# Causal attention: the value step by groups of four query tiles instead of pairs

## The chip, the cores and the metric

The kernel runs on one core of one Trainium2 chip. The metric is the device time of one execution in microseconds; the kernel before stands at 2201.59 us, the median of 3 runs.

## The reference

One layer of a decoder: a half-step feed-forward block, one input projection, three branches (spatial gating, causal multi-head attention, attention into a memory), a gated merge, and a second half-step feed-forward block. Batch 1, 1024 positions, model width 1024, all in float32. The change touches only the causal attention, which has 8 heads with queries and keys of 96 and values of 64 columns:

```python
def causal_block_attention(q, k, v):
    ...
    scale = Dqk ** -0.5
    ...
        s = jnp.einsum('bqhd,bkhd->bhqk', qi, k).astype(jnp.float32) * scale
        qpos = i * Q_BLOCK + jnp.arange(Q_BLOCK)
        mask = kpos[None, :] <= qpos[:, None]
        s = jnp.where(mask[None, None], s, NEG)
        p = jax.nn.softmax(s, axis=-1)
        return jnp.einsum('bhqk,bkhd->bqhd', p.astype(v.dtype), v)
```

## The kernel before, in words

**Precision.** A float32 operand of a matmul is split into a high part `hi` (a cast on ScalarE, ACT, line 127) and a low part `lo` (a subtraction on VectorE, DVE, line 128) by `split`. A product of two split operands is three matmuls on TensorE, PE (`mm3`, lines 144 to 146). The value step is an exception: the 128 stationary columns of `vv` hold the high and the low part of a head's 64 value columns side by side, so that two matmuls do, one with the high and one with the low part of the probabilities, and two halves of the result are added afterwards.

**Tiles.** The 1024 positions are 8 tiles of 128. A head is worked in four steps j = 0 to 3 of two query tiles each, i = 2j and 2j + 1, and all eight heads follow one another; the stage lies at about 1286 to 1431 us of the profiled span.

- `scores(h, j)`, line 838: for each of the two query tiles, `mm3` against the keys that the mask allows, into a tile `mm` of two PSUM banks; on DVE a reduction that adds the mask, takes the maximum and writes the scores to SBUF as `pr0` to `pr7` (line 857: a custom instruction of 128 x 128(i + 1) and a short one that reads the accumulator into `a_mx`); on ACT the exponential in place (line 863), which also leaves the row sums in `a_rs`. There is one buffer for each `pr`.
- `turn(h, j)`, line 867: the probabilities are transposed on PE (line 879), up to four tiles of 128 x 128 into one PSUM bank, and split (line 885) into buffers `whi` and `wlo`. Step j has j + 1 such blocks, each with two key tiles times two query tiles. In the last block one of the four tiles lies beyond the mask: it isn't transposed, and POOL writes zeros there (line 884).
- `value(h, j)`, line 889: 2j + 2 key tiles, for each a matmul with the high and one with the low part, 256 moving columns each (lines 894 and 895), accumulated in a bank. ACT copies one half of the result to `ysum` (line 902), DVE adds the other half (line 903). After every second step of an odd head four query tiles of two heads are complete: DVE takes the reciprocal of the row sums (`a_inv`, line 908), POOL spreads it, PE transposes it (line 914), ACT copies it (916), POOL multiplies (917), and the result is split (919).
- `prepare(h + 1)`, line 823: the next head's queries and keys are transposed (line 415, tiles `aq` and `ak`), four transposes to a block, and split with a gain (lines 136 and 137).

**Buffers.** PSUM has 8 banks: `bank` is a pool of four (turned blocks, prepare, value sums, transposed reciprocals), and `mm` has two tiles of two banks. `whi` and `wlo` have five buffers each, with room for two blocks in each.

**Order.** Each engine works through its instructions in order, and the program's order is the order in which this code calls the functions, refined by a scheduler that places the instructions of nearby calls by estimated times. Step n of the loop (line 925) calls `scores` of step n, up to two blocks of `prepare`, `turn` of step n - 1 and `value` of step n - 2.

Of the kernel before, what the change touches and what calls it, by code (L numbers as in the profile page):

```python
# [8 lines left out]
F32 = mybir.dt.float32  # L9
# [7 lines left out]
P = 128  # L17
# [3 lines left out]
NT = S // P  # L21
# [4 lines left out]
H = 8  # L26
# [16 lines left out]
class Kernel:  # L43
# [756 lines left out]
    def attention(self):  # L800

        nc, tc = self.nc, self.tc
# [12 lines left out]
        yt, st, qkt, pair, ysum, inv = [], {}, {}, {}, {}, {}  # L815
        with tc.tile_pool(name="att", bufs=1) as p:
# [50 lines left out]
            def turn(h, j):  # L867
                prs, out = st[h, j], []
                for c in range(j + 1):
                    if c % 2 == 0:  # L870
                        hi, lo = (self.wide(n).rearrange("p (c q) -> p c q", c=2) for n in ("whi", "wlo"))
                    b = self.bank()

                    order = (2 * c + 1, 2 * c)
                    for s, kk in enumerate(order):
                        for t in range(2):
                            if kk <= 2 * j + t:
                                at = (2 * s + t) * P
                                nc.tensor.transpose(b[:, at:at + P], prs[t][:, kk * P:(kk + 1) * P], self.ident)  # L879
                    dst = hi[:, c % 2], lo[:, c % 2]  # L880
                    z = P if c == j else 0
                    if z:
                        for x in dst:
                            nc.gpsimd.memset(x[:, :z].bitcast(F32), 0.0)
                    self.split(dst[0][:, z:], dst[1][:, z:], b[:, z:])
                    out += [(kk, tuple(x[:, s * 2 * P:(s + 1) * 2 * P] for x in dst)) for s, kk in enumerate(order)]
                st[h, j] = out

            def value(h, j):
                o = self.bank()[:, :2 * P]  # L890
                pts = st.pop((h, j))
                for n, (kk, pt) in enumerate(pts):
                    w = vv[kk][:, h].rearrange("p s d -> p (s d)")
                    nc.tensor.matmul(o, w, pt[0], start=n == 0, stop=False)  # L894
                    nc.tensor.matmul(o, w, pt[1], start=False, stop=n == len(pts) - 1)  # L895
                own = h % 2 * VD
                rows, other = slice(own, own + VD), slice(VD - own, 2 * VD - own)
                if h % 2 == 0 and j % 2 == 0:
                    ysum[h // 2, j // 2] = p.tile([P, 4 * P], F32, name="ysum", bufs=3)
                ys = ysum[h // 2, j // 2]  # L900
                y = ys[rows, j % 2 * 2 * P:(j % 2 + 1) * 2 * P]
                nc.scalar.copy(y, o[other])
                nc.vector.tensor_tensor(y, y, o[rows], op=ALU.add)
                if h % 2 and j % 2:
                    b = self.bank()
                    w = self.row()
                    rs = self.small.tile([P, 2, 4], F32, name="a_inv", tag="a_inv")
                    nc.vector.reciprocal(rs, inv[h // 2][:, :, 2 * (j - 1):2 * (j + 1)])
# [9 lines left out]
                    cols = slice((j - 1) * 2 * P, (j + 1) * 2 * P)  # L918
                    self.split(yt[h // 2][0][:, cols], yt[h // 2][1][:, cols], ys)

            steps = [(h, j) for h in range(H) for j in range(NT // 2)]
# [3 lines left out]
            for n in range(len(steps) + 2):  # L925
                if n < len(steps):
                    h, j = steps[n]
                    scores(h, j)
                    if j == 0 and h + 1 < H:
                        ahead = prepare(h + 1)  # L930
                    for _ in range((0, 2, 1, 2)[j]):
                        next(ahead, None)
                if 0 <= n - 1 < len(steps):
                    turn(*steps[n - 1])
                if n >= 2:
                    value(*steps[n - 2])
# [999 lines left out]
```

## Time and profile before

| | |
|---|---|
| runs | 2201.34, 2201.59, 2202.05 us |
| median | 2201.59 us |
| span of the profiled execution | 2198.6 us |
| the profiled execution's own time | not given beside its span; the median of the runs lies 3.0 us above the span |
| PE, busy share of the span | 99% |
| DVE | 70% |
| ACT | 41% |
| POOL | 11% |

"Busy" counts an engine's instructions and not its waits. PE's instructions overlap, so that their durations add up to more than the time they take; what one of them costs is read from the distance between starts. An operand is written as out<-in by the program's names, with partitions x elements behind it. A row of a group of instructions ends with the idle time ahead of them and with the instruction that ended most of it. A row of the timeline has the time from the span's start, the duration, the engine, the line, and how many equal instructions stand together. In the table of stretches each engine has its busy time and, in brackets, its instructions; the last three numbers are PE's granted clock, the share of DMA and GB/s.

### The profile page before, as it was taken

To read this page: it belongs to the slowest core of one execution; us is meant where nothing else is said; L and a number is where in the kernel's file an instruction comes from. 1 tells how busy PE (TensorE), PEld (TensorE's weight loads), DVE (VectorE), ACT (ScalarE), POOL (GpSimd) and SP (SyncE) were. 2 spreads that over 40 slices of the span, in tenths; PEclk is the share of its full clock that TensorE was granted. 3 is DMA by queue.
4 is the path that set the end of the run, shared out by engine and by line. 5 is a ranking of instruction groups with operands and counts; after the bars stand their busy time and mean duration, and the time that the engine had idled before them with its cause. 6 is when DMAs were issued, how large, how long until landed. Compare 5 with 4: busy or idle time off the path is not lost.

```text
span 2198.6 us, 27597 instructions
## 1 busy us (share of the span) xinstructions
PE 2181.6 (99%) x10304; PEld 1819.9 (83%) x10304; DVE 1549.2 (70%) x2415; ACT 896.7 (41%) x1501; POOL 243.8 (11%) x246
## 2 busy tenths in 40 slices
PE   9999999999999999999999999999999999999999
PEld 5788888888887888898888889988888888888887
DVE  7966666679889555467466769885886666657884
ACT  5422222243455333444244559843432222234332
POOL 0012112100000000022000221140011111210000
PEclk9999999999999999999999999999999999999999
DMA  4242333385432333225151541094033333338543
GB/s 145 82 146 99 96 101 115 133 306 172 133 114 96 125 106 125 94 92 172 55 190 58 218 175 43 17 332 166 29 124 100 99 109 101 115 116 299 170 130 106
DMA packets 113062, 285.92 MB, mean 130 GB/s; under 512 B 13344, under 2 KB 21664, under 8 KB 112800
## 3 DMA queue, kind: packets, MB, share of 16 engines
q1 hardware_dynamic: 112928, 284.16, 38.0%
q8 instruction: 81, 1.33, 0.2%
q14 instruction: 53, 0.43, 0.1%
HBM read 201.80 MB, written 82.31 MB: 129 GB/s over the span
## 4 chain that ended last, share of the span: by engine, by line
PE 93%; DVE 5%; ACT 1%; issue 1%; DMA 0%; SPq 0%; ACTq 0%; DVEq 0%
PE bank L144 13%; PE bank L145 13%; PE bank L146 13%; PE one L144 13%; PE one L145 13%; PE one L146 13%; PE mm L146 3%; PE mm L144 3%; PE mm L145 3%; PE bank L879 1%; PE bank L415 1%; PE bank L894 1%; PE bank L895 1%; DVE wlo L133 1%; PE one L1579 1%
## 5 line engine op out<-in xcount | busy, mean ns | idle before, releaser
L132 ACT CAST whi<-x 128x1024 fp32r<-128x1024 f32 (+1 forms) x189 | 179.5, 952 | 469.8 <-PE one L145 206.8
L1283 DVE TENSOR_TENSOR t<-t,one 128x512 f32<-128x512 f32 x178 | 122.2, 686 | 229.5 <-PE one L146 228.7
L144 PE MATMUL bank<-h,whi 128*128 128x512 f32 x644 | 250.9, 390 | 0.0
L145 PE MATMUL bank<-h,whi 128*128 128x512 f32 x644 | 250.7, 389 | 0.0
L146 PE MATMUL bank<-h,wlo 128*128 128x512 f32 x644 | 250.5, 389 | 0.0
L133 DVE TENSOR_TENSOR wlo<-x,whi 128x1024 fp32r<-128x1024 f32 (+1 forms) x189 | 226.2, 1198 | 28.6 <-ACT whi L132 28.5
L144 PE MATMUL one<-h,whi 128*128 128x512 f32 x476 | 186.2, 391 | 0.7 <-ACT t L1392 0.7
L146 PE MATMUL one<-h,wlo 128*128 128x512 f32 x476 | 185.2, 389 | 0.0
L145 PE MATMUL one<-h,whi 128*128 128x512 f32 x476 | 185.2, 389 | 0.0
L127 ACT CAST whi<-w 128x1024 fp32r<-128x1024 f32 (+1 forms) x108 | 95.1, 899 | 143.4 <-PE one L145 62.7
L128 DVE TENSOR_TENSOR wlo<-w,whi 128x1024 fp32r<-128x1024 f32 (+1 forms) x108 | 110.1, 1033 | 60.5 <-ACT whi L127 60.4
L144 PE MATMUL one<-w,whi 128*128 128x512 f32 x392 | 152.5, 389 | 0.0
L145 PE MATMUL one<-w,whi 128*128 128x512 f32 x392 | 152.5, 389 | 0.0
L146 PE MATMUL one<-w,wlo 128*128 128x512 f32 x392 | 152.5, 389 | 0.0
L1680 POOL TENSOR_TENSOR raw<-raw 128x512 f32<-128x512 f32 x38 | 62.6, 1647 | 804.3 <-DVE raw L1526 804.3
L146 PEld LDWEIGHTS bank<-h,wlo 128*128 128x128 f32 x644 | 120.9, 188 | 25.1
L144 PEld LDWEIGHTS bank<-h,whi 128*128 128x128 f32 x644 | 120.9, 188 | 24.9
L145 PEld LDWEIGHTS bank<-h,whi 128*128 128x128 f32 x644 | 120.9, 188 | 24.8
L144 PE MATMUL bank<-whi 128*128 128x512 f32 x352 | 136.9, 389 | 0.0
L145 PE MATMUL bank<-wlo,whi 128*128 128x512 f32 x352 | 136.9, 389 | 0.0
L146 PE MATMUL bank<-whi,wlo 128*128 128x512 f32 x352 | 136.9, 389 | 0.0
L128 DVE TENSOR_TENSOR wlo<-h,whi 128x512 fp32r<-128x512 f32 x130 | 88.2, 714 | 25.7 <-ACT whi L127 25.7
(381 smaller groups left out, 5040.1 us busy)
## 6 DMA issues: line engine op xcount, KB each, us to landing
x<-in_ffn_w_gu_dram SPq DMA_DIRECT2D x78, 512.0 KB, 5.1
w<-tdt SPq DMA_DIRECT2D x40, 512.0 KB, 4.8
tdb<-raw SPq DMA_DIRECT2D x64, 256.0 KB, 2.1
h<-in_ffn_w_down_dram SPq DMA_DIRECT2D x64, 256.0 KB, 6.0
w<-tdb SPq DMA_DIRECT2D x30, 512.0 KB, 4.5
tdt<-w SPq DMA_DIRECT2D x48, 256.0 KB, 2.1
gate<-raw SPq DMA_DIRECT2D x23, 512.0 KB, 2.6
tdt<-raw SPq DMA_DIRECT2D x40, 256.0 KB, 2.9
```

The source lines that it names most:

```text
L127: self.nc.scalar.copy(hi, src)
L128: return (eng or self.nc.vector).tensor_tensor(lo, src, hi.bitcast(F32), op=ALU.subtract)
L132: self.nc.scalar.copy(hi, src)
L133: return lambda: self.nc.vector.tensor_tensor(lo, src, hi.bitcast(F32), op=ALU.subtract)
L144: mmul(out, s[0], m[0], start=first, stop=False, **kw)
L145: mmul(out, s[0], m[1], start=False, stop=False, **kw)
L146: self.last = mmul(out, s[1], m[0], start=False, stop=last, **kw)
L415: nc.tensor.transpose(b[:m, k * P:(k + 1) * P], s, self.ident)
L879: nc.tensor.transpose(b[:, at:at + P], prs[t][:, kk * P:(kk + 1) * P], self.ident)
L894: nc.tensor.matmul(o, w, pt[0], start=n == 0, stop=False)
L1283: return self.nc.vector.tensor_tensor(out, x, y, op=ALU.add)
L1680: sub = lambda d, x, y: (eng or nc.gpsimd).tensor_tensor(d, x, y, op=ALU.subtract)
```

## The change

`turn` and `value` now work on groups g of four query tiles (4g to 4g + 3) in place of pairs. `blocks(g)` lists what is turned together into one bank: for each of the key tiles 0 to 4g, all four query tiles (512 columns); then key tile 4g + 1 for the query tiles 1 to 3 together with key tile 4g + 3 for query tile 3 (384 + 128 columns); then key tile 4g + 2 for the query tiles 2 and 3 (256 columns). Group 1 has seven blocks, named b0 to b6 below, group 0 has three, b0' to b2'. Nothing beyond the mask is stored, so the zeros go. The value matmuls take 512 columns, or 384, 256 or 128 where the mask cuts. The sum of a group stays in one bank, which may be kept from one call of `value` to the next. `ysum` is copied and added in 512 columns.

A step j of head h now calls, behind `scores` and `prepare`: for j = 0 the blocks b0 to b2 of the head before; for j = 1 its b3 to b6 and the value matmuls of its first four key tiles; for j = 2 the rest of these, and the three blocks of head h's group 0; for j = 3 the value matmuls of group 0. Per head 36 transposes and ten splits of turned probabilities stay; the value matmuls of all eight heads fall from 320 to 192.

```diff
@@ -812,7 +812,7 @@
                     src = raw[:, t].rearrange("p (x o d) -> p x o d", o=2, d=VD)[:, :, o]
                     d = v.rearrange("p (x o) s d -> p x o s d", o=2)[:, :, o]
                     self.split(d[:, :, o], d[:, :, 1 - o], src)
-        yt, st, qkt, pair, ysum, inv = [], {}, {}, {}, {}, {}
+        yt, st, qkt, pair, ysum, inv, ptt, acc, room = [], {}, {}, {}, {}, {}, {}, {}, []
         with tc.tile_pool(name="att", bufs=1) as p:
             self.causal_mask(p)
 
@@ -864,48 +864,52 @@
                         pr[:, :n], pr[:, :n], ACT.Exp, bias=mx[:, t:t + 1], scale=-1.0, accum_out=rs[:, t:t + 1])
                 st[h, j] = prs
 
-            def turn(h, j):
-                prs, out = st[h, j], []
-                for c in range(j + 1):
-                    if c % 2 == 0:
-                        hi, lo = (self.wide(n).rearrange("p (c q) -> p c q", c=2) for n in ("whi", "wlo"))
-                    b = self.bank()
-
-                    order = (2 * c + 1, 2 * c)
-                    for s, kk in enumerate(order):
-                        for t in range(2):
-                            if kk <= 2 * j + t:
-                                at = (2 * s + t) * P
-                                nc.tensor.transpose(b[:, at:at + P], prs[t][:, kk * P:(kk + 1) * P], self.ident)
-                    dst = hi[:, c % 2], lo[:, c % 2]
-                    z = P if c == j else 0
-                    if z:
-                        for x in dst:
-                            nc.gpsimd.memset(x[:, :z].bitcast(F32), 0.0)
-                    self.split(dst[0][:, z:], dst[1][:, z:], b[:, z:])
-                    out += [(kk, tuple(x[:, s * 2 * P:(s + 1) * 2 * P] for x in dst)) for s, kk in enumerate(order)]
-                st[h, j] = out
-
-            def value(h, j):
-                o = self.bank()[:, :2 * P]
-                pts = st.pop((h, j))
-                for n, (kk, pt) in enumerate(pts):
+            def blocks(g):
+
+                return [[(kk, 0, 0)] for kk in range(4 * g + 1)] + [
+                    [(4 * g + 1, 1, 0), (4 * g + 3, 3, 3 * P)], [(4 * g + 2, 2, 0)]]
+
+            def turn(h, g, some):
+                prs, out = st[h, 2 * g] + st[h, 2 * g + 1], ptt.setdefault((h, g), [])
+                for n in some:
+                    if n % 2 == 0:
+                        room[:] = [self.wide(x).rearrange("p (c q) -> p c q", c=2) for x in ("whi", "wlo")]
+                    b, at = self.bank(), 0
+                    for kk, t0, at in blocks(g)[n]:
+                        for t in range(t0, 4):
+                            nc.tensor.transpose(b[:, at:at + P], prs[t][:, kk * P:(kk + 1) * P], self.ident)
+                            at += P
+                    dst = [x[:, n % 2] for x in room]
+                    self.split(dst[0][:, :at], dst[1][:, :at], b[:, :at])
+                    out += [(kk, t0, [x[:, c:c + (4 - t0) * P] for x in dst]) for kk, t0, c in blocks(g)[n]]
+
+            def value(h, g, n=None):
+                pts, total = ptt[h, g], 4 * g + 4
+                if (h, g) not in acc:
+                    acc[h, g] = self.bank(), []
+                o, done = acc[h, g]
+                for kk, t0, pt in pts[:n]:
                     w = vv[kk][:, h].rearrange("p s d -> p (s d)")
-                    nc.tensor.matmul(o, w, pt[0], start=n == 0, stop=False)
-                    nc.tensor.matmul(o, w, pt[1], start=False, stop=n == len(pts) - 1)
+                    for x in pt:
+                        done.append(nc.tensor.matmul(
+                            o[:, t0 * P:], w, x, start=not done, stop=len(done) == 2 * total - 1))
+                del pts[:n]
+                if len(done) < 2 * total:
+                    return
+                del acc[h, g]
                 own = h % 2 * VD
                 rows, other = slice(own, own + VD), slice(VD - own, 2 * VD - own)
-                if h % 2 == 0 and j % 2 == 0:
-                    ysum[h // 2, j // 2] = p.tile([P, 4 * P], F32, name="ysum", bufs=3)
-                ys = ysum[h // 2, j // 2]
-                y = ys[rows, j % 2 * 2 * P:(j % 2 + 1) * 2 * P]
+                if h % 2 == 0:
+                    ysum[h // 2, g] = p.tile([P, 4 * P], F32, name="ysum", bufs=3)
+                ys = ysum[h // 2, g]
+                y = ys[rows]
                 nc.scalar.copy(y, o[other])
                 nc.vector.tensor_tensor(y, y, o[rows], op=ALU.add)
-                if h % 2 and j % 2:
+                if h % 2:
                     b = self.bank()
                     w = self.row()
                     rs = self.small.tile([P, 2, 4], F32, name="a_inv", tag="a_inv")
-                    nc.vector.reciprocal(rs, inv[h // 2][:, :, 2 * (j - 1):2 * (j + 1)])
+                    nc.vector.reciprocal(rs, inv[h // 2][:, :, 4 * g:4 * g + 4])
                     for o in range(2):
                         d = rs[:, o].unsqueeze(2)
                         nc.gpsimd.tensor_copy(
@@ -915,25 +919,32 @@
                     w = self.row()
                     nc.scalar.copy(w, b)
                     nc.gpsimd.tensor_tensor(ys, ys, w, op=ALU.mult)
-                    cols = slice((j - 1) * 2 * P, (j + 1) * 2 * P)
+                    cols = slice(g * 4 * P, (g + 1) * 4 * P)
                     self.split(yt[h // 2][0][:, cols], yt[h // 2][1][:, cols], ys)
 
-            steps = [(h, j) for h in range(H) for j in range(NT // 2)]
             ahead = prepare(0)
             for _ in ahead:
                 pass
-            for n in range(len(steps) + 2):
-                if n < len(steps):
-                    h, j = steps[n]
-                    scores(h, j)
-                    if j == 0 and h + 1 < H:
-                        ahead = prepare(h + 1)
-                    for _ in range((0, 2, 1, 2)[j]):
-                        next(ahead, None)
-                if 0 <= n - 1 < len(steps):
-                    turn(*steps[n - 1])
-                if n >= 2:
-                    value(*steps[n - 2])
+            for h in range(H + 1):
+                for j in range(NT // 2):
+                    if h < H:
+                        scores(h, j)
+                        if j == 0 and h + 1 < H:
+                            ahead = prepare(h + 1)
+                        for _ in range((0, 2, 1, 2)[j]):
+                            next(ahead, None)
+                    if h and j == 0:
+                        turn(h - 1, 1, range(3))
+                    elif h and j == 1:
+                        turn(h - 1, 1, range(3, 7))
+                        value(h - 1, 1, 4)
+                    elif j == 2:
+                        if h:
+                            value(h - 1, 1)
+                        if h < H:
+                            turn(h, 0, range(3))
+                    elif j == 3 and h < H:
+                        value(h, 0)
         return yt
 
     def mixer(self, norm):

```

The scheduler's order moves with it. Three places follow, each as one engine's rows in the order of the program; "x2" stands for two equal instructions in a row.

On DVE, between the first and the last reduction of the query tiles 4 to 7 of one head, after the change (`pr_10998` to `pr_11083` are the tiles pr4 to pr7; the splits `wlo` are those of the turned blocks of the head before, `x_10477` the attention's result, `h_10943` a prepared key or query):

```order
L907 TENSOR_TENSOR ysum<-ysum,bank 64x512
L128 TENSOR_TENSOR wlo<-bank,whi 128x512 x3
L857 ISA pr_10998,a_mx<-mm,mask 128x640
L857 ISA a_mx 128x1
L128 TENSOR_TENSOR x_10477<-ysum,x_10476 128x512
L857 ISA pr_11007,a_mx<-mm,mask 128x768
L857 ISA a_mx 128x1
L137 SCALAR_TENSOR_TENSOR h_10943<-bank,g_ev_k,h_10942 96x512
L128 TENSOR_TENSOR wlo<-bank,whi 128x512 x3
L857 ISA pr_11074,a_mx<-mm,mask 128x896
L857 ISA a_mx 128x1
L857 ISA pr_11083,a_mx<-mm,mask 128x1024
```

The same engine and place before the change (`pr_11093` to `pr_11155` are pr4 to pr7, the splits are those of the same head's tiles 2 to 5):

```order
L903 TENSOR_TENSOR ysum<-ysum,bank 64x256
L857 ISA pr_11093,a_mx<-mm,mask 128x640
L857 ISA a_mx 128x1
L857 ISA pr_11102,a_mx<-mm,mask 128x768
L857 ISA a_mx 128x1
L128 TENSOR_TENSOR wlo<-bank,whi 128x512 x2
L857 ISA pr_11146,a_mx<-mm,mask 128x896
L857 ISA a_mx 128x1
L128 TENSOR_TENSOR wlo<-bank,whi 128x512
L128 TENSOR_TENSOR wlo<-bank,whi 128x384
L857 ISA pr_11155,a_mx<-mm,mask 128x1024
L857 ISA a_mx 128x1
```

Before, pr4 and pr5 are reduced one behind the other; after, splits of group 1 of the head before stand ahead of pr4, between pr4 and pr5 and between pr5 and pr6. Since the turned blocks of that group read its old pr4 to pr7, the new pr4 can be written only when the transposes of b0 to b4, which read the old one, are done.

On PE, at the end of a head's group 1 after the change (`h_10418` to `h_10421` are the value columns of the key tiles 4 to 7, `pr_10655` to `pr_10701` the tiles pr0 to pr3 of the next head, `aq` its successor's queries):

```order
L894 MATMUL bank<-whi,h_10418 128x512
L415 MATMUL bank<-ident,aq 96x128 x4
L894 MATMUL bank<-wlo,h_10418 128x512
L894 MATMUL bank<-whi,h_10419 128x384
L894 MATMUL bank<-wlo,h_10419 128x384
L894 MATMUL bank<-whi,h_10421 128x128
L894 MATMUL bank<-wlo,h_10421 128x128
L894 MATMUL bank<-whi,h_10420 128x256
L880 MATMUL bank<-ident,pr_10655 128x128
L880 MATMUL bank<-ident,pr_10661 128x128
L880 MATMUL bank<-ident,pr_10695 128x128
L880 MATMUL bank<-ident,pr_10701 128x128
```

The end of a value step of query tiles 4 and 5 on PE before (the same names; `h_10541` to `h_10544` are the next keys and queries):

```order
L894 MATMUL bank<-whi,h_10419 128x256
L895 MATMUL bank<-wlo,h_10419 128x256
L894 MATMUL bank<-whi,h_10418 128x256
L895 MATMUL bank<-wlo,h_10418 128x256
L415 MATMUL bank<-ident,ak 96x128 x4
L144 MATMUL mm<-h_10543,h_10541 128x512
L145 MATMUL mm<-h_10544,h_10541 128x512
L146 MATMUL mm<-h_10543,h_10542 128x512
```

After the change the value matmuls of one head stand in long runs, with the widths 512, 384, 128 and 256 at the end, and the transposes of b0' (key tile 0 for pr0 to pr3) follow them; before, runs of value matmuls of 256 columns alternate with scores.

On DVE at the end of the last head after the change (`pr_12196` and `pr_12205` are pr6 and pr7):

```order
L857 ISA pr_12196,a_mx<-mm,mask 128x896
L857 ISA a_mx 128x1
L128 TENSOR_TENSOR wlo<-bank,whi 128x256
L857 ISA pr_12205,a_mx<-mm,mask 128x1024
L857 ISA a_mx 128x1
L912 RECIPROCAL a_inv<-a_rs 128x8
L128 TENSOR_TENSOR wlo<-bank,whi 128x512 x2
L907 TENSOR_TENSOR ysum<-ysum,bank 64x512
L128 TENSOR_TENSOR wlo<-bank,whi 128x256
```

The same place before (`pr_12417` and `pr_12426` are pr6 and pr7):

```order
L857 ISA pr_12417,a_mx<-mm,mask 128x896
L857 ISA a_mx 128x1
L903 TENSOR_TENSOR ysum<-ysum,bank 64x256
L857 ISA pr_12426,a_mx<-mm,mask 128x1024
L857 ISA a_mx 128x1
L128 TENSOR_TENSOR wlo<-bank,whi 128x384
L908 RECIPROCAL a_inv<-a_rs 128x8
L903 TENSOR_TENSOR ysum<-ysum,bank 64x256
L128 TENSOR_TENSOR wlo<-bank,whi 128x512
L128 TENSOR_TENSOR wlo<-bank,whi 128x384
```

The reciprocal stood behind one split of the last head and now stands directly behind the last reduction, ahead of all the splits of group 1 and of the add of `ysum`.

## The prediction, made before the changed kernel ran

> **What bounds the kernel now.** I read the page first, for the engine that carries the end.
> ```profile
> span 2198.6 us, 27597 instructions
> PE 2181.6 (99%) x10304; PEld 1819.9 (83%) x10304; DVE 1549.2 (70%) x2415; ACT 896.7 (41%) x1501; POOL 243.8 (11%) x246
> PE 93%; DVE 5%; ACT 1%; issue 1%; DMA 0%; SPq 0%; ACTq 0%; DVEq 0%
> ```
> PE carries 93% of the chain that ended last, so a microsecond saved on PE is a microsecond of time, provided PE stays fed. Averages over the whole kernel say little about the attention, so I next read the table of stretches for two windows inside it (columns: length, then busy time and instructions of PE, PEld, DVE, ACT, POOL, then granted clock and DMA).
> ```profile
> 1340.00:1360.00 20.00, 20.00 (x151) 18.89 (x151) 18.37 (x43) 16.84 (x38) 3.56 (x11) 1.00 0.03 13
> 1400.00:1420.00 20.00, 19.98 (x151) 18.62 (x151) 18.31 (x42) 17.26 (x41) 3.74 (x15) 1.00 0.01 2
> ```
> Here PE has no gap, but DVE is busy 92% and ACT 84 to 86%. This is the point on which the whole prediction turns: the stage is bound by PE with almost no slack on the two engines that feed it. The clock is 1.00 and no DMA matters.
>
> **What one instruction costs.** PE's matmuls overlap, so their price is the distance from start to start in the timeline, not the duration.
> ```profile
> 1394.75 1.80 PE L879 MATMUL bank<-ident,pr 128*128 128x128 f32 x15
> 1396.31 0.48 PE L144 MATMUL mm<-h,h 96*128 96x512 f32 x1
> 1396.62 0.40 PE L145 MATMUL mm<-h,h 96*128 96x512 f32 x1
> 1396.86 0.39 PE L146 MATMUL mm<-h,h 96*128 96x512 f32 x1
> 1397.08 0.34 PE L144 MATMUL mm<-h,h 96*128 96x384 f32 x1
> 1397.26 0.34 PE L145 MATMUL mm<-h,h 96*128 96x384 f32 x1
> ...
> 1399.00 0.28 PE L894 MATMUL bank<-whi,h 128*128 128x256 f32 x1
> 1399.12 0.28 PE L895 MATMUL bank<-wlo,h 128*128 128x256 f32 x1
> ```
> A matmul of 512 columns takes 0.23 us (1396.62 to 1396.86, to 1397.08), one of 384 takes 0.175 (1397.08 to 1397.26, rounded), one of 256 takes 0.12. The 15 transposes take 1.56 us, and the matmul behind them holds the next one 0.08 longer than usual (0.31): (1.56 + 0.08) / 15 = 0.11 each.
>
> **The change on PE: fewer, wider value matmuls.** Before, a head's value step has 2 + 4 + 6 + 8 = 20 key tiles, each with a hi and a lo matmul of 256 columns: 320 in all, 320 x 0.12 = 38.4 us. After, a head has 12 key tiles: six of 512 columns and two each of 384, 256 and 128. That is 96 x 0.23 = 22.1, 32 x 0.175 = 5.6, 32 x 0.12 = 3.8, and 32 of 128 columns, which the trace before doesn't have.
> ```profile
> L895 PEld LDWEIGHTS bank<-wlo,h 128*128 128x128 f32 x136 | 25.9, 190 | 0.1
> ```
> No row fits, so I bound it: at least 0.06 (half of the 256-column matmul), at most 0.19 (the whole weight load, if nothing hid it). I take 0.11, the transposes' spacing, the nearest row with 128 columns and a weight load of its own: 3.5 us. The sum is 35.0, a gain of **3.4 us** on PE (5.0 and 0.8 at the ends). The Trainium skill (TensorE: Matmul & The Clock Gate, Back-to-back issue gap) gives about 81 ns for a weight load and matmul pair of 128 columns, which would make the gain 4.3. The same place gives 131 ns for 512 columns, where this trace has 230, so I don't lean on it.
>
> The transposes stay 36 per head, and the scores are untouched. So per head PE has before: 56 transposes (36, 16 of prepare, 4 of the sums) x 0.11 = 6.2, scores 18 x 0.23 + 6 x 0.175 + 12 x 0.12 = 6.6, value 4.8, together 17.6; after, 17.2.
>
> **The change on DVE, ACT and POOL.**
> ```profile
> L128 DVE TENSOR_TENSOR wlo<-bank,whi 128x512 fp32r<-128x512 f32 x41 | 26.9, 677 | 2.1 <-POOL wlo L884 2.1
> L127 ACT CAST whi<-bank 128x512 fp32r<-128x512 f32 x41 | 22.6, 578 | 0.1
> L128 DVE TENSOR_TENSOR wlo<-bank,whi 128x384 fp32r<-128x384 f32 x27 | 14.7, 545 | 0.0
> L903 DVE TENSOR_TENSOR ysum<-ysum,bank 64x256 f32<-64x256 f32 x26 | 10.8, 415 | 1.6 <-ACT ysum L902 0.8
> L902 ACT COPY ysum<-bank 64x256 f32<-64x256 f32 x26 | 9.5, 366 | 4.3 <-PE bank L895 3.2
> ```
> A head has ten splits of turned probabilities before and after, and 4608 columns in both (6 x 512 + 4 x 384; now 8 x 512 + 2 x 256): no change. The memsets on POOL go; the first row says that DVE waited 2.1 us for them in 120, beside a PE without gaps, so I cost them at nothing. The 32 copies and adds of ysum become 16 of twice the width. By the pair 384 to 512 the step of 128 columns is 0.13 us on DVE, so an add of 512 takes about 0.415 + 0.26 = 0.68, and DVE saves 2 x 0.415 - 0.68 = 0.15 each, 2.4 us in all; ACT about as much. That is 0.3 us per head on engines with about 1.5 to spare: useful, but PE doesn't wait for their sum, it waits for their order.
>
> **The order, which is the real question.** Before, a step turns two query tiles; turning, value and scores alternate finely. After, seven blocks of group 1 (b0 to b6) are turned in one go beside steps 0 to 2 of the next head, three blocks (b0' to b2') of group 0 in step 2. I walked PE, ACT and DVE by hand through the order of the changed program with these rows; t = 0 is the first score of query tile 4 of an odd head.
> ```profile
> 1341.26 0.81 DVE L857 CUSTOM_DVE_ANT_0 pr<-mm,mask 128x640 f32<-128x640 f32 x1
> 1342.00 0.08 DVE L857 DVE_READ_ACCUMULATOR2_ANT a_mx<- 128x1 f32 x1
> ...
> 1342.67 0.94 DVE L857 CUSTOM_DVE_ANT_0 pr<-mm,mask 128x768 f32<-128x768 f32 x1
> 1343.55 0.08 DVE L857 DVE_READ_ACCUMULATOR2_ANT a_mx<- 128x1 f32 x1
> 1343.55 1.74 DVE L128 TENSOR_TENSOR wlo<-bank,whi 128x512 fp32r<-128x512 f32 x3
> 1345.21 1.08 DVE L857 CUSTOM_DVE_ANT_0 pr<-mm,mask 128x896 f32<-128x896 f32 x1
> ```
> So pr4 holds DVE 0.74, pr5 0.88 and a split 0.57.
>
> *Place 1, tiles 4 to 7.* PE issues scores and b0, b1 until 2.98, b2 until 3.42, then a prepare and b3, b4, b5 until 5.18. Tile 6's scores need the PSUM that pr4's reduction empties, tile 7's that of pr5. ACT's cast of b2 ends at 4.2, DVE's split of b2 at 4.8, pr4 at 5.6 and, behind one more split, pr5 at 7.0. PE is ready for them at 5.18 and 6.39: it loses 0.7. DVE couldn't take pr4 first: the tile pr4 is single, and its old contents are read by the transposes of b0 to b4, so the new reduction has to stand behind b4. This wait is new; before, a pr tile was turned two steps before it was overwritten. Behind it in DVE's queue stand pr5 and the splits of b3 to b5, whose banks PE wants back. In an even head the splits come sooner, pr4 waits for b4 until 4.6, and PE loses 0.4.
>
> *Place 2, the turn of the head.* PE runs 23 value matmuls and transposes for which DVE has little to do; DVE idles 0.9 to 1.9 us until the scores of tiles 0 and 1 arrive at 14.3. Then it has pr0, pr1, ysum (behind ACT's copy), the split of b0', pr2 and the split of b1', about 2.9 us until 17.3, while PE has 2.3 us of other work. Group 0's value waits: 0.7 lost in an odd head, 0.4 in an even one.
>
> So PE loses 1.4 and 0.8, 1.1 in the mean. The Trainium skill (TensorE: Matmul & The Clock Gate, Architectural detail) says that ACT and DVE are strict FIFOs and that PE only pulls weight loads forward; by that rule none of these engines steps round its own wait, as the walk assumes. If they could, only the 3.4 would be left.
>
> **The sum.** The same point of heads 1 and 7, the last scores and the first matmul of the next stage before:
> ```profile
> 1304.21 0.48 PE L144 MATMUL mm<-h,h 96*128 96x512 f32 x1
> ...
> 1410.66 0.40 PE L144 MATMUL mm<-h,h 96*128 96x512 f32 x1
> ...
> 1431.39 0.40 PE L144 MATMUL bank<-x,whi 128*128 128x512 f32 x1
> ```
> (1410.66 - 1304.21) / 6 = 17.74 a head, 0.15 above PE's own work. After: 17.2 + 1.1 = 18.25, so **+3.0 us** in six heads. *Head 0:* tile 4 of head 1 comes 0.9 us sooner, since seven transposes (0.8) now lie behind it: **-0.9**. *The tail,* from tile 4 of head 7 to the last value matmul: before 1431.39 - 1410.66 = 20.7. After, 8.5 to the end of the scores, then 44 transposes (4.8) and value matmuls (7.5), 12.3 us of work with nothing else to issue. Group 0's value waits 1.1 there, because DVE's reciprocal stands ahead of its splits and needs the exponentials of pr7. The run b0 to b6 loses 1.3: seven blocks with 0.57 us of DVE against 0.44 of PE, in four banks. That is 23.2: **+2.5**. Sum +4.6, and 0.4 for PE's restarts after waits, which the walk leaves out: +5.0. Against the profiled execution the span becomes 2203.6; the median of the runs lies 3.0 above the span before (2201.59), so **2206.6**, told as 2206.5. What follows the attention on PE is the same work, with its DMAs issued as before.
>
> **The rivals.**
> *A, PE stays fed (the other side).* Two score buffers, four banks and the lighter ysum work cover both places, as they cover the bursts now; for it speaks that PE shows no gap in 20 us before at 92% DVE. Then only the matmuls count: -3.4, and the 0.15 of waits per head may go too, -1.2: 2197.0 (2195.4 with 0.06 for 128 columns). The point that decides: pr4 must be read 0.5 us earlier, at t = 5.2, when PE has issued b5.
> *B, the change doesn't save what it says.* The 128-column matmuls cost a whole weight load, 0.19, and the gain is 0.8: 2201.6 + 5.0 + 2.6 = 2209. Against it: 256-column matmuls run at 0.12 with the same load hidden.
> *C, DVE sets the pace.* Losses at both places double, since each late split delays the next reduction: 1.1 more in seven heads, 2214. For it speaks only that DVE has 92% now.
>
> **How the numbers follow.** Forecast 0.50, A 0.30, B 0.08, C 0.12. A measurement of this kernel can tell about 0.2%, 4.4 us: below 2197.2 is faster, above 2206.0 slower. The forecast, with an error of 3 us in the walk, gives 0.18 same and 0.32 slower; A 0.13 faster and 0.17 same; B 0.02 and 0.06; C slower. Together 0.13, 0.37, 0.50. The forecast's own range is 2203 to 2210. For 8 in 10 the range takes in most of A and of C: 2196.5 to 2213.
>
> **What would show it.** In the changed profile: value matmuls of 512 columns 0.23 apart and those of 128 about 0.11; PE idle in the attention, a few tenths at a time, ended by DVE's a_mx (place 1) and by wlo (place 2), 1.1 us a head together; DVE's idle time before pr0 of each head ended by PE; the tail longer by 2 us or more, with a wait of DVE for ACT's pr at the reciprocal. If PE shows no such idle time, A is right; if the waits are for the weight load at 128 columns, B; if DVE is at 97% or more, C. The prediction fails if the order was chosen well enough that the two places cover each other.

## The result, and the profile after

The changed kernel takes **2207.70 us**, the median of 8 runs (2205.70 to 2208.24), against 2201.71 before (8 runs, 2200.68 to 2202.05): 1.0024 times as long, 95% interval 1.0015 to 1.0034. The forecast was 2206.5, with 2196.5 to 2213.0 as its range. The page of the profiled execution after, from its first part and from the chain that ended last:

```profile
span 2206.5 us, 27187 instructions
PE 2185.3 (99%) x10176; PEld 1814.0 (82%) x10176; DVE 1546.3 (70%) x2399; ACT 894.2 (41%) x1485; POOL 232.5 (11%) x182
PE 92%; DVE 5%; ACT 1%; issue 1%; DMA 0%; SPq 0%; ACTq 0%; DVEq 0%
```

PE has 128 instructions fewer and is busy 3.7 us longer. One thing must be taken out first: in this execution PE's clock was granted at 0.91 in the stretch 60 to 80 us, where before it was 1.00, and the attention, ahead of which nothing was changed, begins 2.38 us later. (The eight runs show the same: four of 2205.70 to 2205.91 us at a mean clock of 1.000, four of 2207.63 to 2208.24 at 0.998 or 0.999.) So I compare the attention alone: from the first transposes of its first head to the first matmul of the next stage. After, in the timeline of PE:

```profile
1288.35 0.60 PE L415 MATMUL bank<-ident,ak 128*96 128x128 f32 x4
...
1305.06 0.48 PE L144 MATMUL mm<-h,h 96*128 96x512 f32 x1
...
1417.47 0.48 PE L144 MATMUL mm<-h,h 96*128 96x512 f32 x1
...
1439.28 0.39 PE L144 MATMUL bank<-x,whi 128*128 128x512 f32 x1
```

The stage took 1431.39 - 1285.97 = 145.42 us before and takes 1439.28 - 1288.35 = **150.93**: 5.5 us more. What follows is equally long in both (767.2 us). The two rows in the middle are the first scores of query tile 4 of heads 1 and 7: (1417.47 - 1305.06) / 6 = 18.73 us per head, against 17.74. The table of stretches at the places shown of before:

```profile
1340.00:1360.00 20.00, 19.18 (x126) 16.97 (x125) 17.98 (x41) 16.94 (x38) 1.52 (x5) 1.00 0.23 80
1400.00:1420.00 20.00, 19.29 (x125) 16.34 (x123) 17.44 (x38) 16.81 (x37) 2.71 (x4) 1.00 0.10 27
```

PE, without a gap before, is now idle 0.7 to 0.8 us in 20, and DVE is busy less (87 to 90%), not more. A busier DVE is not the cause; it must be when its results come.

**The value matmuls** did become cheaper, in the timeline of PE by their starts:

```profile
1378.25 0.40 PE L894 MATMUL bank<-wlo,h 128*128 128x512 f32 x1
1378.49 0.34 PE L894 MATMUL bank<-whi,h 128*128 128x384 f32 x1
1378.67 0.34 PE L894 MATMUL bank<-wlo,h 128*128 128x384 f32 x1
1378.84 0.22 PE L894 MATMUL bank<-whi,h 128*128 128x128 f32 x1
1378.90 0.28 PE L894 MATMUL bank<-wlo,h 128*128 128x128 f32 x1
1379.01 0.33 PE L894 MATMUL bank<-whi,h 128*128 128x256 f32 x1
1379.18 0.28 PE L894 MATMUL bank<-wlo,h 128*128 128x256 f32 x1
```

512 columns take 0.24, 384 take 0.17 to 0.18, and the two of 128 columns 0.06 and 0.11, 0.085 each. But the matmul behind these two, the first of 256 columns, holds the next one 0.17 in place of 0.12, in all 16 places. With 0.231, the median distance behind the 96 matmuls of 512, that makes 96 x 0.231 + 32 x 0.175 + 16 x 0.17 + 16 x 0.12 + 32 x 0.085 = 35.1 us, 3.3 less than before. The Trainium skill (TensorE: Matmul & The Clock Gate, Back-to-back issue gap) has about 81 ns for 128 columns, which is near the 85 of these two by themselves, without what they cost the matmul behind. Its 131 ns for 512 this trace doesn't bear out (231).

**Place 1**, tiles 4 to 7, in heads 4 (even) and 5 (odd), on PE:

```profile
1363.92 1.84 PE L880 MATMUL bank<-ident,pr 128*128 128x128 f32 x12
1365.84 0.50 PE L144 MATMUL mm<-h,h 96*128 96x512 f32 x1
1366.18 0.40 PE L145 MATMUL mm<-h,h 96*128 96x512 f32 x1
...
1367.02 0.34 PE L146 MATMUL mm<-h,h 96*128 96x384 f32 x1
1367.32 0.50 PE L144 MATMUL mm<-h,h 96*128 96x512 f32 x1
...
1383.83 0.82 PE L880 MATMUL bank<-ident,pr 128*128 128x128 f32 x6
1384.80 0.50 PE L144 MATMUL mm<-h,h 96*128 96x512 f32 x1 [0.16 <-DVE a_mx L857]
```

In brackets the view gives idle time and its releaser, but only what lies behind the modelled end of the matmul ahead, and nothing for short gaps. The distances show more. Twelve transposes from 1363.92 would end their issue at 1365.24 (12 x 0.11); tile 6's scores start at 1365.84, 0.60 late. That is two waits. The first one is inside the row of twelve, which at 1.84 is about 0.36 too long: its last four, those of block b5, start at 1365.11 and not at about 1364.80, since b5 gets the PSUM bank of b2, which DVE's split empties only at 1365.05. The other 0.25 is tile 6's own wait for pr4. Tile 7's scores are 0.13 late. In the odd head tile 6's scores are 1384.80 - 1384.49 = 0.31 late. And the first matmul behind each wait holds the next one 0.34 instead of 0.23: **a restart costs 0.11 more**. DVE just then, in the even and in the odd head:

```profile
1364.36 0.69 DVE L128 TENSOR_TENSOR wlo<-bank,whi 128x512 fp32r<-128x512 f32 x1 [0.78 <-ACT whi L127]
...
1383.92 0.82 DVE L857 CUSTOM_DVE_ANT_0 pr<-mm,mask 128x640 f32<-128x640 f32 x1 [0.68 <-PE bank L880]
```

In the odd head DVE itself waits 0.68 us ahead of pr4, and what it waits for is PE's transposes: the forecast wait of the new pr4 for the old one's readers. In the even head it waits 0.78 us for ACT's cast of b2, and ACT had waited 0.99 us for PE's transposes of b2. So DVE's results are late although DVE stands idle just ahead of them. What closes too late is a loop: PE transposes, ACT casts, DVE subtracts, and only then has PE the bank or the tile again.

**Place 2**, the turn of the head, in the odd head 5, first on DVE, then on PE, then in the even head 4 on PE:

```profile
1374.70 0.29 DVE L857 CUSTOM_DVE_ANT_0 pr<-mm,mask 128x128 f32<-128x128 f32 x1 [1.44 <-PE mm L146]
...
1375.37 0.69 DVE L907 TENSOR_TENSOR ysum<-ysum,bank 64x512 f32<-64x512 f32 x1
1376.10 0.69 DVE L128 TENSOR_TENSOR wlo<-bank,whi 128x512 fp32r<-128x512 f32 x1
1376.70 0.55 DVE L857 CUSTOM_DVE_ANT_0 pr<-mm,mask 128x384 f32<-128x384 f32 x1
...
1377.18 1.02 DVE L128 TENSOR_TENSOR wlo<-bank,whi 128x512 fp32r<-128x512 f32 x2
```

```profile
1374.62 0.38 PE L880 MATMUL bank<-ident,pr 128*128 128x128 f32 x2
1375.05 0.44 PE L144 MATMUL mm<-h,h 96*128 96x384 f32 x1
1375.33 0.34 PE L145 MATMUL mm<-h,h 96*128 96x384 f32 x1
...
1376.38 0.60 PE L415 MATMUL bank<-ident,ak 128*96 128x128 f32 x4
1376.85 0.64 PE L415 MATMUL bank<-ident,aq 128*96 128x128 f32 x4
1377.92 0.50 PE L894 MATMUL bank<-whi,h 128*128 128x512 f32 x1 [0.43 <-DVE wlo L128]
```

```profile
1355.49 0.49 PE L146 MATMUL mm<-h,h 96*128 96x256 f32 x2
1356.21 0.64 PE L415 MATMUL bank<-ident,ak 128*96 128x128 f32 x4 [0.23 <-DVE wlo L128]
```

DVE idles 1.44 us, then has pr0, pr1, ysum, a split, pr2 and a split. PE's eight transposes from 1376.38 would be issued by 1377.26; group 0's value starts 0.66 later, behind the *second* split. The first split, b0', ended at 1376.79. Why the second? The program gives the value sum the PSUM bank that b1' used, and DVE's subtraction of b1' is what empties it. In the even head, transposes of prepare wait in the same way for the bank of b0': the second matmul of the row ahead starts at 1355.70 (its end, 1355.98, less 0.28) and takes 0.12, and the transposes come 0.39 later.

### The profile page after: what moved, and what is told of

It is laid out like the page before. It is cut to its first block, busy times and chain, and to the rows that moved or that the text cites. A ratio compares the mean times of both kernels' runs of the same rounds, so it can differ in the third digit from the quotient of the medians.

```text
span 2206.5 us, 27187 instructions
## 1 busy us (share of the span) xinstructions
PE 2185.3 (99%) x10176; PEld 1814.0 (82%) x10176; DVE 1546.3 (70%) x2399; ACT 894.2 (41%) x1485; POOL 232.5 (11%) x182
## 4 chain that ended last, share of the span: by engine, by line
PE 92%; DVE 5%; ACT 1%; issue 1%; DMA 0%; SPq 0%; ACTq 0%; DVEq 0%
PE bank L144 13%; PE bank L145 13%; PE bank L146 13%; PE one L144 13%; PE one L145 13%; PE one L146 13%; PE mm L144 3%; PE mm L146 3%; PE mm L145 2%; PE bank L894 1%; PE bank L880 1%; PE bank L415 1%; DVE wlo L133 1%; PE one L1590 1%; DVE pr L857 1%
```

## The experiments

In the table, "start" and "next" are the first transposes of the first head and the first matmul of the next stage, from PE's timeline of each run; all times in us. What follows the attention is 767.1 to 767.7 us in every run. Each ratio is against the executions of before that were taken beside the run. The length of the attention is read from one execution of each kernel; the same waits return there in each pair of heads (that ahead of group 0's value is 0.43 us in heads 3, 5 and 7 of the changed kernel), so it shows smaller differences than the medians, which also hold what happens ahead of the stage.

| run | median of its runs | ratio to before, 95% | start | next | attention |
|---|---|---|---|---|---|
| before | 2201.71 | | 1285.97 | 1431.39 | 145.42 |
| changed | 2207.70 | 1.0015 to 1.0034 | 1288.35 | 1439.28 | 150.93 |
| exact_pairs | 2201.51 | 0.9990 to 1.0007 | 1286.03 | 1430.47 | 144.44 |
| after_hi | 2198.01 | 0.9974 to 0.9991 | 1286.02 | 1428.32 | 142.30 |
| before_hi | 2204.01 | 1.0002 to 1.0019 | 1286.24 | 1434.65 | 148.41 |
| pr4_two | 2204.76 | 1.0008 to 1.0026 | 1285.90 | 1435.48 | 149.58 |
| value_whole | 2203.94 | 1.0003 to 1.0021 | 1285.98 | 1434.36 | 148.38 |
| turn_early | 2208.32 | 1.0021 to 1.0046 | 1286.19 | 1438.28 | 152.09 |
| cols_256 | 2207.52 | 1.0017 to 1.0038 | 1286.04 | 1437.99 | 151.95 |
| value0_late | 2209.00 | 1.0023 to 1.0048 | 1287.10 | 1439.39 | 152.29 |
| whole_and_two | 2205.15 | 1.0007 to 1.0025 | 1288.23 | 1437.33 | 149.10 |
| before_three_banks | 2228.89 | 1.0106 to 1.0135 | 1286.69 | 1458.80 | 172.11 |
| fine_groups | 2204.80 | 1.0006 to 1.0024 | 1288.25 | 1435.82 | 147.57 |

The theory: PE's value work fell, and the coarser order makes PE wait for DVE. The main rival: PE's own work grew somewhere, by weight loads that are no longer hidden or by restarts of another cause.

**Does PE wait for DVE?** after_hi takes the suspected cause away:

```diff
-                    self.split(dst[0][:, :at], dst[1][:, :at], b[:, :at])
+                    nc.scalar.copy(dst[0][:, :at], b[:, :at])
```

(with one buffer `whi` standing for both parts).

> The changed kernel without the low part of the turned probabilities: DVE's 80 subtractions (47 us of its 140 in the stage) go, and the matmuls that took the low part take the high part again, so PE's work is the same. Theory (PE waits for DVE's late results): nearly all of the waits go, 1.3 to 1.5 us per head, and the time falls to 2197 to 2199, below the kernel before. Rival (PE's own work is what grew, through matmuls that don't hide their weight loads or through restarts of another cause): 2205 or more.

2198.01 us. The table of stretches:

```profile
1340.00:1360.00 20.00, 20.00 (x138) 17.96 (x136) 11.91 (x28) 18.13 (x41) 2.78 (x5) 1.00 0.01 2
1400.00:1420.00 20.00, 20.00 (x135) 18.19 (x134) 11.96 (x26) 16.23 (x36) 2.02 (x3) 1.00 0.08 27
```

PE has no gap with the same matmuls, and the attention is 8.6 us shorter than in the changed kernel and 3.1 shorter than before. So the waits are for DVE's results, and the rival falls: PE's own work did shrink. The edit takes work off DVE and at the same time a step out of the loop, so it doesn't tell which of the two PE was waiting for. The same cut in the kernel before:

> The kernel before without the low part of the turned probabilities, as in the run of the changed kernel beside it. Theory: PE hardly waits for DVE there, so that 1 to 2 us go, 2200; the changed kernel in the same form is 3 us faster than this one (PE's own saving). Rival (the kernel before was as bound by DVE as the changed one): 2196 or less, and no difference between the two forms.

It came out *longer*, 2204.01, the attention by 3.0 us: an outright miss. With less DVE work the scheduler orders everything anew, and the new order put another wait in, on PE in the odd heads:

```profile
1370.95 0.36 PE L894 MATMUL bank<-whi,h 128*128 128x256 f32 x1 [0.64 <-ACT t L916]
```

A value sum waits here for ACT's copy of the transposed reciprocals. So the pair of runs doesn't give PE's saving, as I had meant it to; what it shows is that a new order can cost more than the work saved. Whether less DVE work would gain anything where PE hardly waits for DVE it doesn't show.

**What do the matmuls alone bring?** exact_pairs leaves the order of before and only cuts the widths:

```diff
-                    if z:
-                        for x in dst:
-                            nc.gpsimd.memset(x[:, :z].bitcast(F32), 0.0)
...
+                    z = P if kk == 2 * j + 1 else 0
-                    nc.tensor.matmul(o, w, pt[0], start=n == 0, stop=False)
+                    nc.tensor.matmul(o[:, z:], w, pt[0][:, z:], start=n == 0, stop=False)
```

(and the same for the low part; the diagonal key tile comes last).

> The kernel before, with the pairs and their order kept, but without zeros: the last key tile of each step is multiplied in 128 columns in place of 256 (64 matmuls), and POOL's memsets go. Theory (the matmuls became cheaper, the coarser order made PE wait): 64 x (0.120 - 0.085) = 2.2 us less PE work, no new wait, 2199.5 us, and the attention 143.2 us against 145.4. Rival (the exact widths are what costs, since a matmul of 128 columns does not hide its weight load): 64 x (0.19 - 0.12) = 4.5 us more, 2206.

2201.51 us, not told apart from before; the attention 1.0 us shorter, half of what was expected. On PE, by the starts:

```profile
1356.06 0.23 PE L893 MATMUL bank<-whi,h 128*128 128x128 f32 x1
1356.12 0.28 PE L894 MATMUL bank<-wlo,h 128*128 128x128 f32 x1
1356.23 0.45 PE L144 MATMUL mm<-h,h 96*128 96x512 f32 x1
1356.51 0.39 PE L145 MATMUL mm<-h,h 96*128 96x512 f32 x1
```

The two of 128 columns take 0.17 against 0.24, 32 x 0.07 = 2.2 us in all, as expected. But the matmul behind them holds the next one 0.28 in place of 0.23 (1356.23 to 1356.51). In the 18 of 32 places where no transpose follows them this is 0.05 us each, 0.9 in all. So the work falls by about 1.3 us and not by 2.2, and the 1.0 of the stage is nearly that. The rival (a whole weight load each) falls: the two cost 0.22 even with what they leave to the next, against 0.24. This is the quickest kernel of the study that computes everything, but it doesn't beat before by more than the runs scatter.

cols_256 asks whether width as such does anything:

```diff
+                        nc.tensor.matmul(o[:, :2 * P], w, x[:, :2 * P], start=s, stop=e)
+                        done.append(nc.tensor.matmul(o[:, 2 * P:], w, x[:, 2 * P:], start=False, stop=e))
```

> The changed kernel with each value matmul of 512 columns made as two of 256 in the same bank. Theory (a column costs the same in both widths, and only the exact widths save): 96 x (2 x 0.120 - 0.231) = 0.9 us more work, of which a part lies in waits: 0 to 1 us longer. Rival (wide matmuls are what saves, since they hide weight loads and restarts better): 3 us longer or more.

The attention is 1.0 us longer, as the theory had it (the medians of the two kernels, 0.2 us apart, don't show it): a column costs nearly the same in both widths, and the saving comes from the widths cut at the mask.

**Where does it wait: place 1.** pr4_two gives the tile pr4 a second buffer:

```diff
-                    pr = p.tile([P, (i + 1) * P], F32, name=f"pr{i}", bufs=1)
+                    pr = p.tile([P, (i + 1) * P], F32, name=f"pr{i}", bufs=1 + (i == 4))
```

> The changed kernel with two buffers for the tile pr4, so that its new reduction needn't wait for the transposes that read the old contents. Theory of the prediction (at the tiles 4 to 7 the single buffer is what makes the scores of tile 6 wait): PE's wait ahead of tile 6 goes from 0.6 and 0.25 us (even and odd head) to about 0, 0.4 us per head, 2204.5. Rival (pr4 is late because DVE's splits of the blocks stand ahead of it anyway): 2207.5, no change.

The attention is 1.35 us shorter, so the single buffer is a cause, but not all went as the theory had it. In the odd heads the wait ahead of tile 6 is gone; in the even heads it moved from tile 6 and the transposes ahead of it to tile 7, whose scores need the PSUM that pr5 empties. The tile pr5 still has one buffer, and its reduction waits there 0.68 us for PE's transposes. On PE:

```profile
1364.20 0.50 PE L144 MATMUL mm<-h,h 96*128 96x512 f32 x1 [0.73 <-DVE a_mx L857]
```

turn_early reaches for the same by order:

```diff
-                        turn(h - 1, 1, range(3))
+                        turn(h - 1, 1, range(5))
...
-                        turn(h - 1, 1, range(3, 7))
+                        turn(h - 1, 1, range(5, 7))
```

> The changed kernel with b0 to b4 turned in step 0 of the next head and b5, b6 in step 1 (now b0 to b2 and b3 to b6), so that the single pr4 is read earlier without a second buffer. Theory of the prediction (the new pr4 waits for b4): the same gain as with two buffers for pr4, 1.4 us in the attention. Rival (five splits on DVE in one step are as late as before and stand ahead of the reductions of tiles 2 and 3): 0 to 2 us longer.

1.2 us longer, as the rival had it. That the five splits are late too is its reading; the trace also has a new wait of 0.90 us in the tail, for ACT's cast, so the splits aren't shown to be the whole of it.

**Place 2.** value_whole drops the early call, so that group 1's eight key tiles are multiplied in one call:

```diff
                         turn(h - 1, 1, range(3, 7))
-                        value(h - 1, 1, 4)
```

> The changed kernel with all value matmuls of group 1 in one call, in step 2 of the next head; now the first four key tiles are multiplied in step 1, and the sum keeps one of the four banks until step 2. Theory A (the kept bank makes the transposes wait): the wait of 0.4 us per pair of heads ahead of the transposes of prepare goes, and some of those at tile 6, 1.5 to 2.5 us in all. Theory B (DVE's order makes PE wait, and the early value matmuls are work that PE does meanwhile): no gain, 0 to 2 us longer.

The attention is 2.55 us shorter, about what theory A had. But the matmuls weren't moved by it: in both kernels all of group 1's value matmuls stand behind the scores of tile 7, in one run. What moved is which bank group 1's sum gets and the order on DVE at the turn of the head:

```profile
1370.86 0.69 DVE L907 TENSOR_TENSOR ysum<-ysum,bank 64x512 f32<-64x512 f32 x1 [1.47 <-ACT ysum L906]
1371.58 0.29 DVE L857 CUSTOM_DVE_ANT_0 pr<-mm,mask 128x128 f32<-128x128 f32 x1
...
1372.14 1.61 DVE L128 TENSOR_TENSOR wlo<-bank,whi 128x512 fp32r<-128x512 f32 x3
1373.68 0.55 DVE L857 CUSTOM_DVE_ANT_0 pr<-mm,mask 128x384 f32<-128x384 f32 x1
```

ysum now stands ahead of pr0, all three splits ahead of pr2, and on PE group 0's value, at 1373.67, follows the transposes with no wait; the 0.66 us are gone. Group 0's sum still takes the bank of b1', which DVE now empties sooner. Bank and order changed together, so which of the two gained the 2.55 us isn't separated. Of theory A's two signs one came, the wait ahead of prepare's transposes in the even heads went; the waits at place 1 stayed.

value0_late calls group 0's value one step later:

```diff
                         turn(h - 1, 1, range(3))
+                        value(h - 1, 0)
...
-                    elif j == 3 and h < H:
-                        value(h, 0)
```

> The changed kernel with the value matmuls of group 0 called one step later (in step 0 of the next head). Theory (place 2: PE waits for DVE's splits b0' to b2' there): the wait of 0.66 us per pair of heads goes, with its restart, 0.77 x 4 = 3 us, 2204.7. Rival (PE waits for DVE's latency wherever it runs out of other work): the wait turns up at another place, within 1 us of the changed kernel.

1.4 us longer, outside both expectations, though the rival's reading fits: the wait turned up again. The wait ahead of group 0's value is as long as before, now for prepare's subtraction in place of a split:

```profile
1380.69 0.50 PE L894 MATMUL bank<-whi,h 128*128 128x512 f32 x1 [0.43 <-DVE h L137]
```

**Are the two places separate?** whole_and_two has both gainful edits.

> The changed kernel with both single changes that gained: group 1's value matmuls in one call, and two buffers for pr4. The first took 2.6 us off the attention, the second 1.4. Theory (two separate waits, at the turn of the head and at the tiles 4 to 7): both gains add up, 146.9 us for the attention, 2202.3. Rival (one lag of DVE that shows at several places): no more than the larger of the two, 148.4 us, 2203.9. In both cases the kernel before in exact widths, 144.45 us, stays ahead.

149.10 us, 0.7 *more* than with value_whole alone. The gains don't add, as the rival had it: one lag, and an edit moves the place where PE meets it. The 0.7 by itself is small beside the scatter of the runs (2203.32 to 2207.43 and 2202.72 to 2208.39).

**Banks.** before_three_banks takes one of the four away from the kernel before:

```diff
+            held = self.bank()
+            nc.vector.memset(held[:, :1], 0.0)
             ahead = prepare(0)
...
+            nc.scalar.copy(self.row()[:, :1], held[:, :1])
```

> The kernel before with one of the four banks of the attention held by a tile that is written ahead of the first head and read behind the last, so that transposed blocks and value sums share three. Theory A (banks are what both kernels run short of, so that a sum kept over a step is costly): PE waits for the splits that empty a bank, 3 us longer or more. Theory B (the order on DVE decides, and banks have room): less than 1 us.

26.7 us longer. Up to 3.4 us of that, by an estimate (20 x 0.08 + 20 x 0.09), are the clock's: in this execution it was 0.92 in the stretch 1360 to 1380 and 0.91 in 1420 to 1440, where before it was 1.00 in the whole stage. The longest wait in a pair of heads, on PE:

```profile
1376.17 0.36 PE L894 MATMUL bank<-whi,h 128*128 128x256 f32 x1 [2.92 <-DVE wlo L128]
```

Four banks are enough for the fine order and three are not; a turned block's bank comes free only when DVE has subtracted. This is the link between a late split and an idle PE.

**Coarse turning or grouped value?** fine_groups turns by pairs in the steps of before, each pair into its half of the group's columns, and multiplies by groups:

```diff
+                    at = slice(u * P, (u + 2) * P)
+                    if c < j:
+                        dst = [x[:, :, at] for x in rooms[c]]
+                        self.split(*dst, b.rearrange("p (k q) -> p k q", k=2))
...
-                if n >= 2:
-                    value(*steps[n - 2])
+                if n >= 2 and steps[n - 2][1] % 2:
+                    value(steps[n - 2][0], steps[n - 2][1] // 2)
```

> Group value matmuls of 512, 256 and 128 columns and the ysum of 512 as in the changed kernel (key tiles 4g + 1 in 384), but turned by pairs in the steps of the kernel before, each pair's blocks going into its half of the group's columns; the diagonal blocks are split in two pieces, 14 splits per head in place of 10, which adds about 0.5 us of DVE per head. Theory (turning seven blocks in one go is what makes DVE late): the attention takes 144 to 146 us, 2201 to 2202. Rival (the value matmuls of a group in one run are what costs, or DVE's extra half microsecond does): 148 us or more, 2205.

147.57 us, between the two, so neither is clearly right. Against the changed kernel, turning finely gains 3.4 us in spite of more DVE work; against exact_pairs 3.1 us stay lost. Whether those come from the grouped value or from the four extra splits per head stays open; the longest wait that returns in each pair of heads is neither directly, 0.60 us ahead of an odd head's first scores, for ACT's part of `prepare` (line 136).

## Why the prediction held, and where its numbers were off

The mechanism was right: less PE work, eaten up by waits for DVE at the two places that the order showed. after_hi shows the cause, pr4_two the single buffer at place 1, value_whole the turn of the head. The sum was right partly because errors cancelled.

- *PE's value work.* Forecast 3.4 us less, measured 3.3. The 128 columns were priced by the transposes at 0.11; they took 0.085 and cost the matmul behind each pair 0.05, which comes to 0.11 each. That second cost wasn't foreseen, so the agreement is partly luck. Rival B priced them at 0.19 and falls.
- *DVE's ysum.* Forecast 0.68 for the add, and the trace has 0.69. That the memsets went shows nowhere on PE.
- *Six heads.* Forecast +3.0, measured 6 x (18.73 - 17.74) = **+5.9**. This is the term that was mis-sized: 1.1 us of waits per head. Own work is 17.6 - 3.3 / 8 = 17.2, so the waits are 1.5. For a pair of heads the walk had 1.1 at place 1 and 1.1 at place 2. Measured at place 1 in the even head: 0.36 ahead of b5, 0.25 and 0.11 of restart ahead of tile 6, 0.13 and 0.11 ahead of tile 7; in the odd head 0.31 and 0.11; 1.4 together. At place 2: 0.39 in the even head; in the odd one 0.66 and 0.10 ahead of the value and 0.21 and 0.11 ahead of tile 2's scores, 1.5. So the walk found the places and nearly the sizes, had the even and odd head of place 1 the wrong way round, missed two smaller waits (tile 7's and tile 2's), and left out the restarts, 0.5 us per pair, which it had put at 0.4 for the whole stage.
- *Head 0.* Forecast -0.9. Measured 1305.06 - 1288.35 = 16.71 against 1304.21 - 1285.97 = 18.24: -1.5.
- *The tail.* Forecast 23.2, +2.5; measured 1439.28 - 1417.47 = 21.8, +1.1. The waits came as forecast in sum, and so did the reciprocal's hold on DVE:

```profile
1428.15 0.20 DVE L912 RECIPROCAL a_inv<-a_rs 128x8 f32<-128x8 f32 x1 [1.31 <-ACT pr L863]
```

```profile
1424.45 0.39 PE L894 MATMUL bank<-whi,h 128*128 128x512 f32 x1
...
1428.46 0.38 PE L880 MATMUL bank<-ident,pr 128*128 128x128 f32 x2
1429.37 0.50 PE L894 MATMUL bank<-whi,h 128*128 128x512 f32 x1 [0.53 <-DVE wlo L128]
...
1431.62 1.04 PE L880 MATMUL bank<-ident,pr 128*128 128x128 f32 x8
1433.11 2.48 PE L880 MATMUL bank<-ident,pr 128*128 128x128 f32 x14 [0.46 <-DVE wlo L128]
1435.75 0.50 PE L894 MATMUL bank<-whi,h 128*128 128x512 f32 x1 [0.16 <-DVE wlo L128]
```

By the distances, with 0.11 for a transpose, group 0's value is 0.69 late, and the run b0 to b6 loses 0.61 ahead of 1433.11 and 1.10 inside and behind the fourteen: 2.4 us, where the walk had 1.1 + 1.3. What it had too long is the way to the end of the scores: 1424.45 - 1417.47 = 7.0, not 8.5.

The three terms together, 5.9 - 1.5 + 1.1, are the 5.5 measured over the stage, against 5.0 forecast: waits put too low in six heads, and a first head and a tail put too long, nearly cancelled. That is luck. Rival A (PE stays fed) falls, and so does C: DVE is busy less than before.

## What to carry to other kernels

Where an engine without gaps is fed through a few buffers that other engines must empty, a change that makes fewer and larger pieces must be judged by when the feeder's results come, not by the work it saves. The feeder's busy share doesn't tell it either: DVE was 87 to 90% busy, less than before, and stood idle just ahead of the results that came late. Read the order on the feeder between two results that the bound engine needs, and add to each wait the cost of the restart. A new order is also an experiment's own side effect here: taking out DVE work made the kernel before 3 us longer.

## What the runs showed of the hardware

Behind a wait, the first matmul of 512 columns holds the next one 0.34 us in place of 0.23, and one of 384 columns 0.28 in place of 0.175. A pair of matmuls of 128 columns with the same weights takes 0.06 and 0.11, and a matmul that follows it holds the next one 0.05 longer (0.17 in place of 0.12 for 256 columns, 0.28 in place of 0.23 for 512). And one PSUM bank fewer, three in place of four, made a stage of 145 us 26.7 us longer, of which about 3.4 at most, an estimate, were the clock's.
